# A three-mixer transformer block on one core: projections of the third stretch in program order, raw weights loaded a set ahead, and two sets of weights in memory that other data has left

## The chip, the cores and the metric

The kernel runs on one core of a Trainium2 chip. A time is the device time of one execution in microseconds. Of the kernel before, three executions were timed: 2087.23, 2089.68 and 2092.42 us, median 2089.68 us. One more execution was recorded by the profiler; all rows below come from it.

The engines are named as in the profile: PE multiplies matrices and transposes, DVE and ACT work on tiles element by element and empty PSUM, POOL works on tiles in SBUF, SP issues the DMAs.

## The reference, cut to what matters

The block takes 1024 tokens of width 1024. Its first part runs three mixers on the same normed input and merges them with gates; its second part is a gated MLP with a short convolution. Everything is float32.

```python
hn = rms_norm(x, norm_mix_g)
u = hn @ w_in                      # 1024 x 7864: MLA latents, forgetting attention, SSD, gates
y_a = mla_branch(u_mla, ...)       # latents -> q, k, v of 8 heads, rotary tail, chunk-causal softmax
y_b = fox_branch(u_fox, ...)       # q, k normed per head; scores plus differences of cumulated log-sigmoids
y_c = ssm_branch(u_ssm, ...)       # convolution, scan over chunks of 64, times silu(z)
merged = g0 * y_a + g1 * y_b + g2 * y_c
x = x + merged @ w_out
x = x + (silu(gate) * val) @ w_down          # gate, val = split(conv(rms_norm(x) @ w_up))
```

## The kernel before, in words

A float32 product is made of three products of halves: `split` (L142 and L143) writes the high half `h` with ACT and the rest `l` with DVE, and `mm3` (L167) sums high times high, high times low and low times high on PE. The stages follow each other on PE, and in most of them PE is the engine that never rests:

- norm and latents (to about 97 us), which leave the latents of the eight tiles of 128 tokens in `ch` and `cl`;
- MLA projections and forgetting-attention values (to about 226 us). For each token tile `t`: products `q` and `kv`, norms and rotary parts on DVE and POOL, then four groups of transposes (`tp`, L500), each emptied into `sh` by ACT (L503) and into `sl` by DVE (L504) and stored by SP (L507). `sh` and `sl` have two buffers each. Beside them run 16 value units `fxv` (8 token tiles, two sets of 256 columns), each emptied into the tile `fv` (one buffer) and stored (L519);
- what the change calls the third branch (226 to 424 us): four sets of 512 columns, in the order z (first half), forgetting-attention queries, keys, z (second half). `load512` loads a set as four raw pieces (tag `wr`, two buffers) and splits each into `w5h` and `w5l`; two sets fit. Then eight units per set, 24 matmuls of 512 columns each, into the PSUM tile `fx`. A z unit is emptied by a tanh and one DVE instruction (`zt`). A query or key unit takes a square on ACT, a reduction `fss`, thirteen small instructions for the reciprocal root and a product `fqn` on DVE, four transposes on PE, then `fsh` on ACT and `fsl` on DVE (one buffer each) and four stores. `gate_sums` (dt, decays, cumulated sums) and `down_sums` (sums of FFN down weights, on POOL, with loads and stores) lie in between;
- attention with fill-in gate projections, the scan, the merge and `w_out` (to about 1445 us);
- the FFN up projection (to about 1876 us): 22 pairs of column blocks, each as seven products of quarter blocks. `raws(i)` loads the two raw blocks of a pair into the tag `wr` (two buffers), POOL forms the sums S12 and S34 (L1417 to L1421), DVE and ACT split them, and PE runs the banks `ua`, `ub`, `uc`, `ud` (L1322). The right-hand sides need token sums T2, T3, T4, made one after the other in the tile `T3f`. The first four pairs are begun early;
- the down projection to the end.

The order of instructions on an engine is in most stages made by a scheduler in the compiler; a `manual_schedule` region keeps the named engines in the order in which the code is written. In the FFN, PE alone is kept so. In the third branch nothing was. SP issues its DMAs in one queue, and a DMA that waits holds up those behind it.

Of the kernel before, what the change touches and what calls it, by code (L numbers as in the profile page):

```python
# [11 lines left out]
F32 = mybir.dt.float32  # L12
# [30 lines left out]
def block_kernel(ctx: ExitStack, tc: tile.TileContext, x, positions, norm_mix_g, w_in, b_gate,  # L43
# [91 lines left out]
    def uid(s):  # L135
        cnt[0] += 1
        return f"{s}_{cnt[0]}"
# [188 lines left out]
    pmla = ExitStack()  # L326
# [5 lines left out]
    ch = [chp.tile([P, 5, P], F32R, name=f"ch{t}", tag=f"ch{t}") for t in range(NT)]  # L332
    cl = [chp.tile([P, 5, P], F32R, name=f"cl{t}", tag=f"cl{t}") for t in range(NT)]

    with ExitStack() as p0:
# [71 lines left out]
        upp = pmla.enter_context(TP("upp", 1, side="right"))  # L407
# [8 lines left out]
    def load_cols(pool, tag, c0, n, bufs):  # L416

        h = pool.tile([P, NK, n], F32R, name=uid(tag), tag=tag + "h", bufs=bufs)
        l = pool.tile([P, NK, n], F32R, name=uid(tag), tag=tag + "l", bufs=bufs)
        for k in range(0, NK, 2):  # L420
            raw = pool.tile([P, 2, n], F32, name=uid("raw"), tag=tag + "r", bufs=2)
            SY.dma_start(raw, w_inv[:, k:k + 2, c0:c0 + n])
            split(h[:, k:k + 2, :], l[:, k:k + 2, :], raw)
        return h, l

    with ExitStack() as pm:
        fvp = pm.enter_context(TP("fvp", 1))
# [6 lines left out]
        def rope(eng, dst, src, t, n):  # L434

            c = cos[:, t:t + 1, :].to_broadcast([P, n, 16])
            s = sin[:, t:t + 1, :].to_broadcast([P, n, 16])
            a, b = src[:, :, 0:16], src[:, :, 16:32]
            t1 = mp.tile([P, n, 16], F32, name=uid("rp1"), tag=f"rp1_{n}", bufs=1)
            t2 = mp.tile([P, n, 16], F32, name=uid("rp2"), tag=f"rp2_{n}", bufs=1)  # L440
            t3 = mp.tile([P, n, 16], F32, name=uid("rp3"), tag=f"rp3_{n}", bufs=1)
            t4 = mp.tile([P, n, 16], F32, name=uid("rp4"), tag=f"rp4_{n}", bufs=1)
            eng.tensor_mul(t1, a, c)
            eng.tensor_mul(t2, b, s)
            eng.tensor_mul(t3, a, s)
            eng.tensor_mul(t4, b, c)
            eng.tensor_sub(dst[:, :, 0:16], t1, t2)
            eng.tensor_add(dst[:, :, 16:32], t3, t4)

        vcols = [load_cols(fvp, "v", C_FQ + 1024, 256, 1)]  # L450
        for t in range(NT):

# [31 lines left out]
            kn = mp.tile([P, 8, 96], F32, name=uid("kn"), tag="kn")  # L484
# [11 lines left out]
            for src, col, dsts in ((qn, gq_col, (q_h, q_l)), (kn, gk_col, (k_h, k_l))):  # L496
                for g in range(2):
                    pt = tps()
                    for j in range(4):
                        T.transpose(pt[:96, j, :], src[:, 4 * g + j, :], ident)  # L500
                    sh = mp.tile([96, 4, P], F32R, name=uid("sh"), tag="sh")
                    sl = mp.tile([96, 4, P], F32R, name=uid("sl"), tag="sl")
                    A.activation(sh, pt[:96, :, :], AF.Copy, scale=col)  # L503
                    V.scalar_tensor_tensor(out=sl, in0=pt[:96, :, :], scalar=col, in1=f32(sh),  # L504
                                           op0=ALU.mult, op1=ALU.subtract)
                    for dst, st in zip(dsts, (sh, sl)):
                        SY.dma_start(dst[4 * g:4 * g + 4, :, t * P:(t + 1) * P].rearrange("h d s -> d h s"), f32(st))  # L507


        for c0 in (0, 256):  # L510
            if c0:
                vcols.append(load_cols(fvp, "v", C_FQ + 1024 + c0, 256, 1))
            vh, vl = vcols[-1]
            for t in range(NT):
                p = acc("fxv", "mv")[:, 0:256]
                mm3(p, tok(hnh, t), tok(hnl, t), lambda k: vh[:, k, :], lambda k: vl[:, k, :], NK)
                vt = fvp.tile([P, 4, P], F32R, name=uid("fv"), tag="fv", bufs=1)
                split(vt[:, :, 0:64], vt[:, :, 64:128], p.rearrange("p (h d) -> p h d", d=64))
                SY.dma_start(fv_d[t * P:(t + 1) * P, c0 // 64:c0 // 64 + 4, :], f32(vt))  # L519
    pmla.close()  # L520
# [18 lines left out]
    V.tensor_add(yv, small, b24.unsqueeze(1).to_broadcast([P, NT, 24]))  # L539
    V.scalar_tensor_tensor(out=yn, in0=yv, scalar=-1.0, in1=yv, op0=ALU.mult, op1=ALU.min)  # L540
    A.activation(e, yn, AF.Exp)
    V.tensor_scalar_add(rec, e, 2.0)
    V.reciprocal(rec, rec)
    V.tensor_mul(s_, e, rec)
    V.tensor_mul(s2, s_, s_)
    V.tensor_scalar_mul(q_, s2, 1.0 / 17)
    for c in (15, 13, 11, 9, 7, 5, 3):
        V.scalar_tensor_tensor(out=q_, in0=q_, scalar=1.0 / c, in1=s2, op0=ALU.add, op1=ALU.mult)
# [66 lines left out]
    with ExitStack() as px:  # L615
# [1090 lines left out]
```

## Time and profile before

| What | us |
|---|---|
| profiled execution, its time | 2090.6 |
| its span in the profile | 2088.9 |
| median of the three timed runs | 2089.68 |
| PE busy in the span | 2019.1 |
| DVE busy in the span | 1402.3 |
| ACT busy in the span | 952.7 |
| POOL busy in the span | 621.7 |

PE is busy for 97% of the span, so the idle time of PE, and the matmuls that run slowly after it, are all that a change of order can win. The table of windows gives, for a stretch of time, the busy time of each engine with its count of instructions, and the clock that PE was granted. The list of waits names what ended each idle stretch of an engine. A matmul of 512 columns is recorded as some 0.39 us long, but the next one starts before it ends; what counts is their pitch, the time from start to start.

### The profile page before, as it was taken

The numbers are of one execution on the slowest core, as the hardware profiler recorded it, in microseconds if no ns is written. First come the engines' busy times: TensorE is split into PE (matmuls) and PEld (weight loads), VectorE is DVE, ScalarE is ACT, GpSimd is POOL, SyncE is SP. The second block draws the span as 40 slices with busy tenths as digits, with TensorE's granted clock in tenths as the row PEclk, the third lists the DMA queues.
The fourth block names the chain that finished last, engine by engine and source line by source line (L and its number), as shares of the span: only waits on it lengthen the run. The fifth ranks groups of instructions, "written<-read, shape, count | busy, mean of one in ns | idle before, by whom it ended". The sixth has DMA issues, their size and how long they took to land.

```text
span 2088.9 us, 29138 instructions
## 1 busy us (share of the span) xinstructions
PE 2019.1 (97%) x10265; PEld 1684.8 (81%) x10265; DVE 1402.3 (67%) x2595; ACT 952.7 (46%) x1739; POOL 621.7 (30%) x606
## 2 busy tenths in 40 slices
PE   6999898999999999999999999999989999999999
PEld 6998687788888888788777888888768888878887
DVE  6687468456666777666987356557887766765665
ACT  5555222145565666554554223323444454444432
POOL 2454122322222222220000030002465455432765
PEclk9999999999999999999999999999999999999999
DMA  5067667754343554324442665431222222229675
GB/s 173 27 182 226 225 222 241 233 154 121 118 130 90 132 157 124 102 81 145 124 132 85 202 205 183 150 123 54 68 91 81 81 81 91 81 93 353 235 227 191
DMA packets 276650, 303.62 MB, mean 145 GB/s; under 512 B 19308, under 2 KB 209784, under 8 KB 276504
## 3 DMA queue, kind: packets, MB, share of 16 engines
q1 hardware_dynamic: 276504, 301.76, 46.7%
q8 instruction: 81, 1.33, 0.3%
q14 instruction: 65, 0.53, 0.1%
HBM read 209.03 MB, written 92.67 MB: 144 GB/s over the span
## 4 chain that ended last, share of the span: by engine, by line
PE 80%; DMA 8%; DVE 6%; ACT 2%; issue 2%; POOL 2%; SPq 0%; ACTq 0%; DVEq 0%; POOLq 0%
PE mm L796 17%; PE dn L1653 9%; PE ybr L167 8%; PE fx L167 5%; PE ua L1322 5%; PE uc L1322 4%; PE ud L1322 4%; PE wo L1368 4%; PE s L886 4%; PE tp L955 2%; PE ub L1322 2%; DMA att_d<-o 2%; PE cq L167 1%; PE q L167 1%; PE o L926 1%
## 5 line engine op out<-in xcount | busy, mean ns | idle before, releaser
L796 PE MATMUL mm<-hnh,wh 128*128 128x512 f32 x576 | 250.4, 435 | 0.0
L796 PE MATMUL mm<-hnh,wl 128*128 128x512 f32 x576 | 226.5, 393 | 0.0
L796 PE MATMUL mm<-hnl,wh 128*128 128x512 f32 x576 | 225.1, 391 | 0.0
L908 POOL TENSOR_SCALAR pm<-pm,rs 128x128 f32<-128x128 f32 (+7 forms) x128 | 107.7, 843 | 351.4 <-DVE rs L907 320.6
L1653 PE MATMUL dn<-dr,dr 128*128 128x512 f32 x592 | 182.3, 389 | 0.0
L961 DVE TENSOR_TENSOR ptl<-tp,pth 128x512 fp32r<-128x512 f32 (+1 forms) x160 | 101.4, 633 | 85.5 <-ACT pth L960 84.6
L891 DVE TENSOR_REDUCE nmx<-s 128x1 f32<-128x128 f32 (+2 forms) x192 | 105.7, 551 | 56.2 <-PE s L889 44.5
L901 ACT ACTIVATE pm<-s,nmx 128x128 f32<-128x128 f32 (+2 forms) x192 | 109.6, 575 | 55.5 <-DVE nmx L898 38.4
L1653 PEld LDWEIGHTS dn<-dr,dr 128*128 128x128 f32 x592 | 111.1, 188 | 22.9
L796 PEld LDWEIGHTS mm<-hnh,wl 128*128 128x128 f32 x576 | 108.1, 188 | 24.8
L796 PEld LDWEIGHTS mm<-hnl,wh 128*128 128x128 f32 x576 | 109.0, 189 | 18.4 <-issue 4.1
L796 PEld LDWEIGHTS mm<-hnh,wh 128*128 128x128 f32 x576 | 108.9, 189 | 17.8 <-issue 4.1
L960 ACT ACTIVATE pth<-tp 128x512 fp32r<-128x512 f32 (+1 forms) x160 | 88.1, 551 | 68.8 <-PE tp L955 68.0
L886 PE MATMUL s<-qk,qk 96*128 96x384 f32 (+5 forms) x480 | 117.6, 350 | 0.9 <-ACT pm L901 0.9
L1238 POOL TENSOR_TENSOR mg<-mg,gl 128x512 f32<-128x512 f32 x16 | 24.8, 1557 | 305.9 <-DVE gl L1235 305.8
L1653 PE MATMUL dn<-dr 128*128 128x512 f32 x296 | 115.3, 390 | 0.1
L142 ACT ACTIVATE wh<-wr 128x1024 fp32r<-128x1024 f32 (+1 forms) x47 | 43.0, 914 | 146.1 <-PE ybr L167 65.0
L167 PE MATMUL fx<-w5h,hnh 128*128 128x512 f32 x256 | 102.1, 403 | 7.6 <-ACT w5h L142 7.6
L143 DVE TENSOR_TENSOR dr<-dr,dr 128x1024 fp32r<-128x1024 f32 x52 | 76.0, 1465 | 49.2 <-ACT dr L142 47.1
L167 PE MATMUL fx<-w5h,hnl 128*128 128x512 f32 x256 | 101.6, 398 | 0.0
L167 PE MATMUL fx<-w5l,hnh 128*128 128x512 f32 x256 | 101.2, 397 | 0.0
L167 PE MATMUL ybr<-al,wh 128*128 128x512 f32 x256 | 99.2, 389 | 0.0
(469 smaller groups left out, 5822.5 us busy)
## 6 DMA issues: line engine op xcount, KB each, us to landing
dr<-act_d SPq DMA_DIRECT2D x99, 256.0 KB
wr<-in_ffn_w_up_dram SPq DMA_DIRECT2D x47, 512.0 KB
wr<-in_w_in_dram SPq DMA_DIRECT2D x36, 512.0 KB
g_d<-t SPq DMA_DIRECT2D x24, 512.0 KB
gl<-g_d SPq DMA_DIRECT2D x24, 512.0 KB
ws<-in_ffn_w_down_dram SPq DMA_DIRECT2D x22, 512.0 KB
wsum_d<-ws SPq DMA_DIRECT2D x22, 512.0 KB
act_d<-fa SPq DMA_DIRECT2D x22, 512.0 KB
```

The costliest lines, as they stand in the source:

```text
L143: return i, le.tensor_sub(l, src, f32(h))
L167: T.matmul(ps, a(k), b(k), start=(i == 0), stop=(i == n - 1))
L796: T.matmul(ps, a[:, k, :], b[half][:, k, :], start=(k == 0 and i == 0), stop=(k == NK - 1 and i == 2))
L886: T.matmul(ps[:, :w], q_[:, qs], k_[:, a:a + w], start=i_ == 0, stop=not last and i_ == len(o.passes) - 1)
L891: later(c + 0.1, lambda ps=ps, ci=ci, a=a, b=b: V.reduce_max(nmx[:, ci:ci + 1], ps[:, :b - a], axis=AX, negate=True))
L901: pss[ci][1][0] = later(c + 0.9 + 0.1 * ci, lambda ci=ci, a=a, b=b: A.activation(p_[:, a:b], pss[ci][0][:, :b - a], AF.Exp, bias=nb, accum ...
L908: G.tensor_scalar(p_[:, 0:n * P], p_[:, 0:n * P], rs[:, 3:4], 0.0, op0=ALU.mult, op1=ALU.add)
L960: later(c + 0.05, lambda th=th, pt=pt, off=off: A.activation(th[:, :off], pt[:, :off], AF.Copy))
L961: pl[0] = later(c + 0.6, lambda th=th, tl=tl, pt=pt, off=off: V.tensor_sub(tl[:, :off], pt[:, :off], f32(th[:, :off])))
L1322: T.matmul(ps, a, b, start=first and n == 0, stop=n == 11, skip_group_check=not first)
L1368: T.matmul(p, a, b, start=k == 0 and i == 0, stop=k == NK - 1 and i == 2)
L1653: T.matmul(ps[m], a[:, ts_], b[:, 512:], start=first_ and j == 0 and q == 0, stop=j == NFH - 1 and q == 2, skip_group_check=not first_)
```

## The change

Nothing that is computed changes. It has five parts.

1. Memory. The latents become four tiles of four token tiles each (`chA`, `chB`, `clA`, `clB`). From token tile 5 on, the split value weights of the second set are written into `chA` and `clA`, whose token tiles 0 to 3 have then been used. `fv` gets two buffers for the first eleven value units.
2. The first set of the third branch. Once the MLA up weights are free (`pup.close()`), a pool `zr` takes their place with four raw buffers for the first z set and four `fv` buffers for the last five value units. The raw pieces are loaded there before those units, and split into the first `w5` set, which lies where the value weights of the first set were, ahead of the branch.
3. The third branch runs in a region in which PE, DVE and ACT are kept in the written order. Its raw pieces now use the four buffers of the tags `wh` and `wl`; the raw pieces of set i+1 are issued at the start of set i, and one piece is split before every odd unit. The transposes of a query or key unit (`turned`) follow two units later; `fsh` and `fsl` have two buffers. `gate_sums` is a generator whose pieces are run one by one between units.
4. FFN: the raw blocks of odd pairs from pair 3 on are loaded into the memory of `T3f` (tag `T3f`), those of the others into `wr` as before.
5. FFN, pair 1: the product `ub` stands ahead of `ud`, not behind the second `uc`.

```diff
-    ch = [chp.tile([P, 5, P], F32R, name=f"ch{t}", tag=f"ch{t}") for t in range(NT)]
-    cl = [chp.tile([P, 5, P], F32R, name=f"cl{t}", tag=f"cl{t}") for t in range(NT)]
+    def four(n):
+        return chp.tile([P, 4, 5, P], F32R, name=uid(n), tag=n)
+    chs, cls = ([four(n + i) for i in "AB"] for n in ("ch", "cl"))
+    ch, cl = ([h[t // 4][:, t % 4] for t in range(NT)] for h in (chs, cls))
...
+    def load512(c0):
+        for k in range(0, NK, 2):
+            if c0 == C_Z:
+                raw = zrp.tile([P, 2, 512], F32, name=uid("raw"), tag="zr", bufs=4)
+            else:
+                raw = f32(fpl.tile([P, 2, 512], F32R, name=uid("raw"), tag=("wh", "wl")[k // 2 % 2]))
+            SY.dma_start(raw, w_inv[:, k:k + 2, c0:c0 + 512])
+            raws.append((k, raw))
...
         for t in range(NT):
+            if t == 5:
+                vcols.append(load_v(*(f32r_halves(four(n)) for n in ("chA", "clA")), 256))
...
+            heads_turn(t, qn, kn)
+        for i in range(NT + 3):
+            values(i % NT, i // NT * 256, fvp.tile([P, 4, P], F32R, name=uid("fv"), tag="fv", bufs=2))
+        pup.close()
+        zrp = pup.enter_context(TP("zr", 1, side="right"))
+        load512(C_Z)
+        for t in range(3, NT):
+            values(t, 256, zrp.tile([P, 4, P], F32R, name=uid("fv"), tag="fv", bufs=4))
     pmla.close()
...
+    for _ in range(NK // 2):
+        split512()
+    pup.close()
...
+        with tc.manual_schedule(engines={mybir.EngineType.PE, mybir.EngineType.DVE, mybir.EngineType.Activation}):
+            for i, which in enumerate((3, 0, 1, 4)):
+                wh, wl = w5[i]
+                for t in range(NT):
+                    if which != 4 and t == 0:
+                        load512({3: C_FQ, 0: C_FQ + 512, 1: C_Z + 512}[which])
+                    if which != 4 and t % 2:
+                        split512()
...
+                    mm3(p, tok(hnh, t), tok(hnl, t), lambda k: wh[:, k, :], lambda k: wl[:, k, :], NK)
+                    if which != 3 or t in (2, 3):
+                        next(gs, None)
+                    if waiting and waiting[0][0] <= units - 2:
+                        turned(*waiting.pop(0)[1:])
...
     def raws(i):
         out_ = []
-        for j in (i, i + NFF):
-            raw = fpl.tile([P, NK, P], F32, name=uid("wr"), tag="wr", bufs=2)
+        if i % 2 and i > 1:
+            two = t3p.tile([P, 2, NK, P], F32, name=uid("wr2"), tag="T3f")
+        for n, j in enumerate((i, i + NFF)):
+            if i % 2 and i > 1:
+                raw = two[:, n]
+            else:
+                raw = fpl.tile([P, NK, P], F32, name=uid("wr"), tag="wr", bufs=2)
...
         product(c0_, hS12, 0, *T1)
+        if n == 1:
+            b0 = bank("ub")
+            product(b0, hS12, 4, *T2)
         d0 = bank("ud")
         product(d0, hS34, 0, *T3)
...
         if n == 1:
             finish_pair(*plain)
-            b0 = bank("ub")
-            product(b0, hS12, 4, *T2)
```

Smaller edits: the rotary step uses two scratch tiles in place of four, and the squares of the key half are written into the tile `kn`, whose place they leave before `kn` is written.

What the compiler makes of it, at three places. The first is DVE at the end of the MLA stage. In the kernel before, the last token tile's four `sl` stand among the value units, then come pieces of `gate_sums` and three more `fv`, and the first split of the third branch follows 18 rows below this excerpt.

```order
L504 SCALAR_TENSOR_TENSOR sl_2701<-tp_2695,gq_col,sh_2700 96x512
L504 SCALAR_TENSOR_TENSOR sl_2712<-tp_2706,gq_col,sh_2711 96x512
L143 TENSOR_TENSOR fv_3101<-fxv_3076,fv_3101 128x4x64
L504 SCALAR_TENSOR_TENSOR sl_2723<-tp_2717,gk_col,sh_2722 96x512
L504 SCALAR_TENSOR_TENSOR sl_2734<-tp_2728,gk_col,sh_2733 96x512
L143 TENSOR_TENSOR fv_3130<-fxv_3105,fv_3130 128x4x64
L579 MEMSET neg 8x128
L603 COPY trim<-tri 128x128
L604 TENSOR_SCALAR trim<-trim 64x128
L143 TENSOR_TENSOR fv_3159<-fxv_3134,fv_3159 128x4x64
```

In the changed kernel, the same engine at the same place (L459 is the old L504):

```order
L143 TENSOR_TENSOR fv_3155<-fxv_3156,fv_3155 128x4x64
L459 SCALAR_TENSOR_TENSOR sl_2575<-tp_2569,gk_col,sh_2574 96x512
L459 SCALAR_TENSOR_TENSOR sl_2586<-tp_2580,gk_col,sh_2585 96x512
L143 TENSOR_TENSOR fv_3184<-fxv_3185,fv_3184 128x4x64
L459 SCALAR_TENSOR_TENSOR sl_2699<-tp_2693,gq_col,sh_2698 96x512
L459 SCALAR_TENSOR_TENSOR sl_2710<-tp_2704,gq_col,sh_2709 96x512
L459 SCALAR_TENSOR_TENSOR sl_2721<-tp_2715,gk_col,sh_2720 96x512
L459 SCALAR_TENSOR_TENSOR sl_2732<-tp_2726,gk_col,sh_2731 96x512
L143 TENSOR_TENSOR w5l_3222<-raw_3060,w5h_3221 128x1024
L143 TENSOR_TENSOR w5l_3222<-raw_3062,w5h_3221 128x1024
```

All value units are emptied first (`fv_3184` is the last), the last token tile's four `sl` come behind them, and the splits of the first z set behind those. On PE the four groups `tp` of that tile stand right in front of the first `fx`.

The second place is DVE in the query units of the third branch. Before, the pieces of two units and of two weight sets are mixed (`w5l_4196` is the set of the keys, `fss` belongs to a unit, `tot` and `F` to `gate_sums`):

```order
L569 TENSOR_TENSOR tot<-tot 128x8 x3
L571 TENSOR_TENSOR F<-pc_3564,tot 128x56
L663 TENSOR_REDUCE fss_3686<-fsq_3684 128x8
L607 COPY cum<-pd_3609 128x128
L665 TENSOR_SCALAR fv_740_3688<-fss_3686 128x8
L143 TENSOR_TENSOR w5l_4196<-raw_4205,w5h_4195 128x1024
L148 TENSOR_SCALAR rs_i_3691<-fv_740_3688 128x8
L151 TENSOR_SCALAR rs_v_3694<-fv_740_3688 128x8
L149 TENSOR_SCALAR fr_741_3690<-rs_i_3691 128x8
L143 TENSOR_TENSOR w5l_4196<-raw_4209,w5h_4195 128x1024
```

Now a unit is finished before the next begins, with one split between two units:

```order
L725 TENSOR_TENSOR fqn_3815<-fx_3718,fr_765_3797 128x512
L143 TENSOR_TENSOR w5l_3648<-raw_3573,w5h_3647 128x1024
L684 SCALAR_TENSOR_TENSOR fsl_3862<-tp_3856,fq_col,fsh_3861 128x512
L719 TENSOR_REDUCE fss_3871<-fsq_3869 128x8
L721 TENSOR_SCALAR fv_782_3873<-fss_3871 128x8
L148 TENSOR_SCALAR rs_i_3876<-fv_782_3873 128x8
```

`fsl_3862` belongs to the unit two before the one whose `fss` follows it.

The third place is PE in pair 1 of the FFN; each row is the first of twelve alike. `wh_15798` holds S12, `wh_15802` S34. Before:

```order
L1322 MATMUL uc_15826<-hnh_13478,wh_15798 128x512
...
L1322 MATMUL ud_15839<-cbh,wh_15802 128x512
...
L1322 MATMUL uc_15826<-hnh_13478,wh_15802 128x512
...
L1322 MATMUL ub_15879<-cbh,wh_15798 128x512
...
L1322 MATMUL ud_15839<-cbh,h_4699_15806 128x512
```

And now, where `wh_15785` is S12 and `wh_15789` is S34:

```order
L1371 MATMUL uc_15813<-hnh_13465,wh_15785 128x512
...
L1371 MATMUL ub_15826<-cbh,wh_15785 128x512
...
L1371 MATMUL ud_15839<-cbh,wh_15789 128x512
...
L1371 MATMUL uc_15813<-hnh_13465,wh_15789 128x512
...
L1371 MATMUL ud_15839<-cbh,h_4693_15793 128x512
```

The product that needs only S12 now stands ahead of the first that needs S34. From the end of the third branch to the FFN, the five engines' orders are the same in both kernels.

More of the change, by code (lines that the diff above doesn't have):

```diff
@@ new lines, in block_kernel, with heads_turn @@
+    raws = []
+    def load512(c0):
[6 more added lines that the diff above has]
+            raws.append((k, raw))
+    def heads_turn(t, qn, kn):
+        for src, col, dsts in ((qn, gq_col, (q_h, q_l)), (kn, gk_col, (k_h, k_l))):
+            for g in range(2):
+                pt = tps()
+                for j in range(4):
+                    T.transpose(pt[:96, j, :], src[:, 4 * g + j, :], ident)
+                sh = mp.tile([96, 4, P], F32R, name=uid("sh"), tag="sh")
+                sl = mp.tile([96, 4, P], F32R, name=uid("sl"), tag="sl")
+                A.activation(sh, pt[:96, :, :], AF.Copy, scale=col)
+                V.scalar_tensor_tensor(out=sl, in0=pt[:96, :, :], scalar=col, in1=f32(sh),
+                                       op0=ALU.mult, op1=ALU.subtract)
+                for dst, st in zip(dsts, (sh, sl)):
+                    SY.dma_start(dst[4 * g:4 * g + 4, :, t * P:(t + 1) * P].rearrange("h d s -> d h s"), f32(st))
@@ L495, in block_kernel @@
                          rq[:, 8:16].unsqueeze(2).to_broadcast([P, 8, 32]))
[L496 to L507, printed above, removed]
@@ L510, in block_kernel @@
[L510 to L519, printed above, removed]
@@ new lines, in block_kernel, with turned @@
+        gs = gate_sums()
+        waiting = []
+        def turned(which, t, qn):
+            pt = tps()
+            for j in range(4):
+                T.transpose(pt[:, j, :], qn[:, 2 * j:2 * j + 2, :].rearrange("p h d -> p (h d)"), ident)
+            col = (fq_col, fk_col)[which]
+            sh = xp.tile([P, 4, P], F32R, name=uid("fsh"), tag="fsh", bufs=2)
+            sl = xp.tile([P, 4, P], F32R, name=uid("fsl"), tag="fsl", bufs=2)
+            A.activation(sh, pt, AF.Copy, scale=col)
+            V.scalar_tensor_tensor(out=sl, in0=pt, scalar=col, in1=f32(sh),
+                                   op0=ALU.mult, op1=ALU.subtract)
+            for dst, st in zip(((fq_h, fq_l), (fk_h, fk_l))[which], (sh, sl)):
+                dv_ = dst.rearrange("(a b) d s -> b d a s", b=2)
+                for b in range(2):
+                    SY.dma_start(dv_[b, 0:64, :, t * P:(t + 1) * P], f32(st[64 * b:64 * b + 64, :, :]))
```

198 lines of the change are left out of this document (95 added, 103 removed).

## The prediction

> **What bounds the kernel now.** I read the page first, then a table of windows, then the waits of PE, and the timeline only where those pointed.
>
> ```profile
> span 2088.9 us, 29138 instructions
> PE 2019.1 (97%) x10265; PEld 1684.8 (81%) x10265; DVE 1402.3 (67%) x2595; ACT 952.7 (46%) x1739; POOL 621.7 (30%) x606
> ```
>
> PE rests for 70 us in all, so no reordering can win more than that and the slow matmuls that follow a rest. The change touches three stretches. In the windows the columns are the length, PE, PEld, DVE, ACT and POOL busy with their instructions, the granted clock, the DMA share and GB/s.
>
> ```profile
> 180.00:220.00 40.00, 32.76 (x256) 30.21 (x255) 23.29 (x53) 16.18 (x29) 10.54 (x18) 1.00 0.78 229
> 220.00:230.00 10.00, 4.28 (x10) 3.41 (x11) 7.70 (x19) 2.87 (x5) 0.00 (x0) 0.52 0.31 97
> 270.00:390.00 120.00, 111.48 (x519) 91.27 (x519) 94.61 (x281) 31.94 (x49) 35.65 (x28) 0.97 0.72 224
> 330.00:340.00 10.00, 8.71 (x41) 6.89 (x39) 5.72 (x18) 1.74 (x3) 3.18 (x3) 1.00 1.00 333
> 340.00:350.00 10.00, 5.42 (x15) 4.48 (x16) 9.72 (x28) 3.77 (x5) 2.73 (x3) 0.66 0.74 228
> 380.00:390.00 10.00, 7.35 (x36) 5.67 (x35) 9.59 (x19) 1.18 (x2) 5.11 (x4) 1.00 0.69 246
> 1475.00:1485.00 10.00, 5.80 (x19) 4.33 (x18) 9.96 (x10) 5.61 (x6) 5.24 (x3) 0.74 0.00 1
> 1485.00:1505.00 20.00, 20.00 (x86) 16.46 (x85) 15.83 (x13) 6.93 (x8) 7.35 (x6) 0.96 0.26 85
> 1505.00:1565.00 60.00, 54.05 (x230) 42.44 (x229) 46.82 (x37) 27.54 (x32) 38.21 (x22) 1.00 0.30 95
> 1565.00:1865.00 300.00, 300.00 (x1323) 247.94 (x1322) 210.35 (x191) 147.26 (x174) 145.25 (x91) 1.00 0.26 83
> ```
>
> PE is idle 7.2 and 5.7 us where the MLA stage ends, 8.5 us in the query and key units (270 to 390), and 4.2 and 6.0 us where the FFN begins. From 1565 on the FFN leaves PE no gap, so nothing is to be won there. The pitch of a warm matmul of 512 columns comes from the chain of waits, where 151 of them follow each other:
>
> ```profile
> 389.96 34.27 PE fx L167 x151
> ```
>
> That is 0.227 us each, 5.45 us for a unit's 24. With it the windows show what a rest costs afterwards. From 220 to 230, ten matmuls took 4.28 us where 2.27 would do: 2.0 us lost at a clock of 0.52. From 340 to 350, fifteen took 5.42 where 3.41 would do: 2.0 lost. From 1475 to 1505, 105 took 25.8 where 23.8 would do: 2.0 lost. After the 2.65 us rest from 380 to 390 the clock stood at 1.00, with nothing lost. So a long rest costs 2 us on top.
>
> The list of PE's waits, of 90 to 440 us and then of 1430 to 1620, says what ended the rests (total, times, longest):
>
> ```profile
> PE fx L167 <- ACT w5h L142: 7.6, 1, 7.6
> PE tp L673 <- DVE fv L665: 5.9, 1, 5.9
> PE fxv L167 <- DVE fv L143: 3.7, 4, 1.5
> PE tp L673 <- DVE fqn L669: 2.6, 1, 2.6
> ...
> PE ud L1322 <- DVE wl L143: 4.2, 1, 4.2
> PE ua L1322 <- ACT cg L1514: 2.6, 1, 2.6
> ```
>
> **Part 1: the end of the MLA stage.** 7.2 + 5.7 + 2.0 = 14.9 us stand there. The timeline shows the reason:
>
> ```profile
> 202.91 0.38 ACT L142 ACTIVATE fv<-fxv 128x256 fp32r<-128x256 f32 x1 [5.20 <-DMA fv_d<-fv]
> ...
> 224.34 0.38 ACT L142 ACTIVATE fv<-fxv 128x256 fp32r<-128x256 f32 x1 [2.77 <-DMA fv_d<-fv]
> 224.62 2.00 ACT L142 ACTIVATE w5h<-raw 128x1024 fp32r<-128x1024 f32 x2
> 226.02 2.35 DVE L143 TENSOR_TENSOR w5l<-raw,w5h 128x1024 fp32r<-128x1024 f32 x2
> ```
>
> A value unit has one `fv`, so each waits until the store of the last has landed, and the first split stands behind the last `fv` on ACT. With two and four buffers these waits go, and the raw z weights have arrived before. But the order of DVE shows what is late next: the last token tile's four `sl` and then the splits. This chain has lain under value units so far:
>
> ```profile
> 201.27 1.03 PE L500 MATMUL tp<-ident,qn 128*96 128x128 f32 x8
> ...
> 203.19 1.25 ACT L503 ACTIVATE sh<-tp,gq_col 96x512 fp32r<-96x512 f32 x2
> 205.25 1.16 SPq L507 DMA_DIRECT2D q_l<-sl  x2
> 208.41 1.52 DVE L504 SCALAR_TENSOR_TENSOR sl<-tp,gk_col,sh 96x512 fp32r<-96x512 f32 x2 [1.65 <-DMA q_l<-sl]
> ```
>
> The key half's `sl` has to wait for the store of the query half, since there are two buffers. From the first transpose to the last `sl` it takes 209.9 - 201.3 = 8.6 us, of which 1.3 were a wait of `sh` for the `fv` ahead of it on ACT, which goes: 7.3. The first split adds half of the 2.35: 1.2. PE itself works 2.1 us of these 8.5 (two rows of 1.03). So a rest of 6.4 us comes back, with 2.0 for the clock after it: 8.4. The part wins 14.9 - 8.4 = 6.5 us. The bounds: 2 us if the 2 MB of raw z weights, which now travel beside the stores (DMA share 0.78), delay them by 4.5 us; 12 us if the stores land so early that a rest of 3 us is left.
>
> [...]
>
> **Part 2: the third branch in written order.** 8.5 us of rests plus the 2.0 after the long one make 10.5. They come from DVE, on which two units and the next weights were mixed (second excerpt of the order): `tp` of L673 waits for `fv` of L665, the start of a chain of small instructions. Now `turned` leaves that chain two units of time, some 12 us: a unit takes PE 5.45 us and its transposes, which the next row prices.
>
> ```profile
> L673 PE MATMUL tp<-ident,fqn 128*128 128x128 f32 x64 | 10.1, 282 | 8.5 <-DVE fv L665 5.9 <-DVE fqn L669 2.6
> ...
> L143 DVE TENSOR_TENSOR w5l<-raw,w5h 128x1024 fp32r<-128x1024 f32 x16 | 20.2, 1265 | 18.9 <-ACT w5h L142 18.9
> L157 DVE TENSOR_TENSOR rs_t<-fr 128x8 f32<-128x8 f32 x48 | 16.5, 344 | 1.5
> L158 DVE TENSOR_TENSOR rs_t<-rs_t,rs_v 128x8 f32<-128x8 f32 x48 | 13.2, 274 | 1.3
> ...
> L159 DVE SCALAR_TENSOR_TENSOR fr<-rs_t,fr 128x8 f32<-128x8 f32 x48 | 8.0, 166 | 1.4
> ```
>
> 10.1 us over 16 units are 0.6, so PE needs 6.05 us a unit, 97 us for 16. DVE was busy 94.6 us between 270 and 390, where these units lay: 98% of that. It fits, barely, and the pieces of `gate_sums` come early in the stretch. I let 3 of the 10.5 us come back as rests and take 7.5, with bounds of 0 (all comes back) and 10.5. Written order also makes DVE wait at each split for a raw piece. That piece is issued a set, some 44 us, ahead, and four buffers hold a set, so these waits have cover; without it a piece would cost its transfer, 6.5 us by the row under the rivals, less the units that PSUM holds in store. The stores have two `fsh` and `fsl` now, which hides them as long as a round trip stays under two units.
>
> **Part 3: the start of the FFN.** 4.2 + 2.0 + 6.0 = 12.2 us. The first rest is that of `ud`, which waits for S34:
>
> ```profile
> 1480.04 2.35 DVE L143 TENSOR_TENSOR wl<-S,wh 128x1024 fp32r<-128x1024 f32 x2
> ...
> 1501.04 1.71 POOL L1417 TENSOR_TENSOR S<-wr 128x512 f32<-128x512 f32 x1 [7.09 <-DMA wr<-in_ffn_w_up_dram]
> ...
> 1537.56 1.62 POOL L1417 TENSOR_TENSOR S<-wr 128x512 f32<-128x512 f32 x1 [6.72 <-DMA wr<-in_ffn_w_up_dram]
> ```
>
> `ub`, 12 x 0.227 = 2.7 us, now runs in that rest, and 1.5 is left, short enough for the clock: 4.7 us won. The 6.0 us later come from raw blocks: POOL stands still until a pair's blocks arrive, as these wait in `wr` for the pair before. With the odd pairs in `T3f`, pair 3 can load once T4 is split, before `wr` is free, and each later pair has the other place. That stall goes; next is DVE, busy 46.8 of 60 us there and 9.96 of 10 ahead of it, so I let 1.2 of the 6.0 come back. The part wins 9.5, with bounds of 4.7 (the blocks help nothing, DVE was the limit) and 12.2.
>
> The smaller edits (two rotary scratch tiles, the squares in `kn`) order POOL, DVE and ACT instructions behind ones that stand before them on the same chain; I price them at nothing. The stages between have the same order as before and shift as a whole.
>
> **The sum.** 6.5 + 7.5 + 9.5 = 23.5 us. The profiled execution took 2090.6 us with a span of 2088.9, so it becomes 2067.1. It lies 0.9 above the median of the three runs, 2089.68, against which the result is measured: 2066. A measurement of this kernel can tell about 0.3%, 6.3 us, from no change.
>
> **The rivals.** First, all of it is won: stores land early and DVE keeps up. The upper bounds give 12 + 10.5 + 12.2 = 34.7 us: 2055. For it speaks that every rest named has its cause removed; against it, that the order puts a bare chain in front of the first `fx`. Chance 0.15.
>
> Second, the FFN blocks help nothing and DVE is the limit there: 6.5 + 7.5 + 4.7 = 18.7 us, 2071. For it speaks the 9.96 of 10 us of DVE ahead; against it the two POOL rows, which wait for a DMA and not for DVE. Chance 0.15.
>
> Third, DVE becomes the bound of the query and key units. L157 takes 344 ns and L159, of the same size, 166; L158 takes 274. Against 166 these excesses are 8.5 and 5.2 us over 48 each, 13.7 in all, and they come from DVE instructions held up while POOL runs `down_sums`. If the written order meets POOL as badly again, twice as much is lost: 13.7 us more on an engine that is 98% full, so the 7.5 of part 2 become -6 and the total 10: 2080. It decides when a unit's DVE work passes 6.05 us. Chance 0.12. [...]
>
> Fourth, slower: the stores of the query and key units become the bound through SP's one queue. ACT and DVE are now in written order, so a `fsl` whose buffer has not landed holds up the whole next unit.
>
> ```profile
> 329.87 6.52 DMA raw<-in_w_in_dram
> ...
> 371.76 4.34 DMA fk_l<-fsl
> ```
>
> A store takes 4.3 us; with two buffers it binds only if the round trip from `fsl` to landing passes 12.1 us. If it stood behind a raw piece and a down-weight load of the same size, 4.3 + 2 x 6.5 = 17.3 us, a unit would take 8.65 us, 2.6 more, 42 us over 16 units: 2066 + 42 = 2108. Below a round trip of 15 us the other gains still outweigh it. Against it: the same bytes go now at a share of 0.72. Chance 0.04.
>
> **Chances and range.** The forecast has 0.54. The first three rivals and the forecast are faster by over 6.3 us; of the third, a quarter (0.03) falls within 0.3%, and 0.03 of the forecast's tails too; slower is the fourth. That gives 0.90 faster, 0.06 same, 0.04 slower. The range from 2055 to 2081 takes in the first three rivals; the forecast's lower bounds together, 2 + 0 + 4.7 us, would be 2083 and are left out.
>
> **What would show it.** Part 1: no `fxv` waits for `fv`, the first `fx` starts near 219 us (225.7 now), waiting for `w5l` or `w5h`, and the waits of `sl` for the store `q_l` stand ahead of it. Part 2: from the first `fx` to the last some 190 us instead of 198.5, no `tp` wait of over 3 us, DVE near full. Part 3: `ud` waits about 1.5 us, the clock stays at 1.00, and POOL's L1417 no longer waits for `wr`. The forecast is wrong if the gap at the first `fx` is as long as before, if query and key units take over 6.3 us each, or if any stage between differs by more than 2 us.

## The result, and the profile after

The changed kernel takes 2073.23 us (median of 4 runs, 2070.47 to 2075.93) beside 2089.61 us before: a ratio of 0.9921, 95% interval 0.9900 to 0.9942. A second series gave 2071.27, 0.9907 (0.9886 to 0.9927); one of its 13 executions of the kernel before took 10963.94 us and is left out of the ratio, and the median of the other twelve is 2090.20 us. The gain is 16.4 and 18.9 us in the two; 23.5 had been forecast, and the range held the time. The profiled execution took 2071.0 us.

Of the page after, the line of busy times: PE does the same work, DVE is busy 23 us longer with as many instructions.

```profile
PE 2014.6 (97%) x10265; PEld 1684.3 (81%) x10265; DVE 1425.6 (69%) x2595; ACT 950.5 (46%) x1739; POOL 616.9 (30%) x606
```

The windows of the changed kernel, the FFN's shifted by the 15 us that it starts earlier (columns as before):

```profile
180.00:220.00 40.00, 33.89 (x266) 32.38 (x264) 27.80 (x64) 19.35 (x38) 16.62 (x35) 0.95 0.85 262
220.00:230.00 10.00, 9.26 (x29) 7.13 (x30) 5.07 (x6) 5.08 (x7) 0.00 (x0) 0.70 0.75 244
...
270.00:390.00 120.00, 117.36 (x557) 96.67 (x556) 98.37 (x286) 32.87 (x52) 38.53 (x28) 1.00 0.75 233
...
1460.00:1470.00 10.00, 8.51 (x37) 6.59 (x36) 9.96 (x10) 5.61 (x6) 5.24 (x3) 1.00 0.38 105
1470.00:1490.00 20.00, 15.50 (x67) 12.17 (x67) 19.96 (x14) 8.49 (x10) 16.84 (x9) 1.00 0.24 79
1490.00:1550.00 60.00, 57.87 (x255) 47.24 (x254) 52.31 (x42) 28.89 (x34) 37.46 (x22) 1.00 0.31 97
```

PE rests 6.9 us around the first `fx` (13.0 before) and 2.6 us in the query and key units (8.5 before). In the FFN the long rest of `ud` is gone, but a new one of 4.5 us stands in the 20 us behind it, where DVE is busy 19.96 of 20 and POOL 16.84. PE's waits name what is late now, from 90 to 440 us and then from 1410 to 1610:

```profile
PE tp L455 <- DVE sl L459: 4.5, 1, 4.5
...
PE fx L167 <- DVE w5l L143: 2.0, 2, 1.4
PE fx L167 <- ACT w5h L142: 1.7, 1, 1.7
...
PE uc L1371 <- ACT e L1585: 5.6, 2, 3.8
PE ud L1371 <- DVE wl L143: 1.5, 1, 1.5
PE ud L1371 <- ACT e L1587: 0.7, 1, 0.7
PE ua L1371 <- ACT cg L1563: 0.3, 1, 0.3
```

No `fxv` waits for `fv` any more, and `ud` waits the 1.5 us that were forecast. The wait of `uc` has grown from 1.7 to 5.6 us; its row in the kernel before (1430 to 1620):

```profile
PE uc L1322 <- ACT e L1533: 1.7, 2, 1.2
```

It waits for ACT's copy of the bank (L1585, the tile `e`), and this copy stands on ACT behind an `fa` of the pair before, which waits for POOL's `cv` (timeline of the changed kernel):

```profile
1483.58 1.24 ACT L1518 ACTIVATE fa<-cv,pc_f 128x1024 f32<-128x1024 f32 x1 [4.90 <-POOL cv L1599]
...
1486.63 0.58 ACT L1585 ACTIVATE e<-uc 128x512 f32<-128x512 f32 x1
```

The stages of every profiled execution, from starts of instructions in its trace: the first `fx`, from it to the last `fx`, when that last one starts, from there to the first `ybr` (attention, no order changed), from the first `ua` to the last `ud`, and from there to the end. Left out is the stretch from the first `ybr` to the first `ua`, 267.7 to 268.5 us in all of them. A row's name says where the kernel differs from the changed one; in its other stages it has the changed kernel's code.

| Kernel | us | first fx | fx | last fx | to ybr | FFN | rest |
|---|---|---|---|---|---|---|---|
| before | 2090.6 | 225.7 | 198.1 | 423.8 | 742.9 | 438.0 | 218.1 |
| changed | 2071.0 | 220.1 | 190.6 | 410.7 | 740.4 | 432.3 | 219.3 |
| changed, again | 2077.1 | 219.4 | 192.5 | 411.9 | 745.3 | 432.3 | 219.7 |
| no FFN part | 2076.9 | 217.5 | 192.6 | 410.1 | 743.1 | 437.3 | 218.0 |
| earlier ub alone | 2074.9 | 216.4 | 194.2 | 410.6 | 741.5 | 435.5 | 219.5 |
| blocks alone | 2073.0 | 217.4 | 192.2 | 409.6 | 742.0 | 434.8 | 218.1 |
| last tile's own memory | 2070.8 | 215.7 | 193.2 | 408.9 | 743.8 | 432.5 | 217.8 |
| no FFN sums | 2063.5 | 219.5 | 191.1 | 410.6 | 742.8 | 422.4 | 219.4 |
| scheduler's order | 2066.2 | 216.0 | 186.8 | 402.8 | 743.0 | 432.3 | 220.2 |
| same, one fsh, fsl | 2074.1 | 219.9 | 191.8 | 411.7 | 741.7 | 432.3 | 220.1 |
| same, late raws | 2071.6 | 215.9 | 191.9 | 407.8 | 744.0 | 432.3 | 219.0 |
| scheduler's order, own memory | 2063.9 | 214.9 | 187.8 | 402.7 | 740.3 | 432.7 | 220.3 |
| no down sums | 2064.2 | 216.6 | 187.9 | 404.5 | 740.9 | 432.3 | 218.5 |
| POOL in order | 2196.8 | 221.4 | 193.3 | 414.7 | 741.3 | 544.0 | 229.1 |

Two things are seen before any experiment is read. The attention, in which no instruction was moved, takes 740.3 to 745.3 us from one execution to the next: that scatter is larger than most differences asked for here, so the experiments are judged by their stage and not by one total. And parts 1 and 2 of the prediction, the end of the MLA stage and the third branch, belong together: of the kernels with the written order and all of POOL's work there, those that reach the first `fx` earlier tend to take longer to the last one (220.1 and 190.6 at one end, 216.4 and 194.2 at the other; POOL in order is the exception).

### The profile page after: what moved, and what is told of

Read it like the earlier page. It is cut to its first block, busy times and chain, and to the rows that moved or that the text cites. A ratio compares the mean times of both kernels' runs of the same rounds, so it can differ in the third digit from the quotient of the medians.

```text
span 2069.3 us, 29096 instructions
## 1 busy us (share of the span) xinstructions
PE 2014.6 (97%) x10265; PEld 1684.3 (81%) x10265; DVE 1425.6 (69%) x2595; ACT 950.5 (46%) x1739; POOL 616.9 (30%) x606
## 4 chain that ended last, share of the span: by engine, by line
PE 84%; DVE 7%; DMA 5%; ACT 2%; issue 2%; SPq 0%; POOL 0%; DVEq 0%; ACTq 0%; POOLq 0%
PE mm L840 17%; PE dn L1703 10%; PE ybr L167 8%; PE ua L1371 5%; PE fx L167 5%; PE ud L1371 5%; PE uc L1371 5%; PE wo L1417 4%; PE s L930 4%; PE tp L999 3%; PE ub L1371 2%; PE fxv L167 1%; PE cq L167 1%; PE o L970 1%; PE kv L167 1%
## 5 line engine op out<-in xcount | busy, mean ns | idle before, releaser
L167 PE MATMUL ybr<-ah,wl 128*128 128x512 f32 x256 | 98.3, 389 | 0.0
```

What stands on the lines that cost most here:

```text
L167: T.matmul(ps, a(k), b(k), start=(i == 0), stop=(i == n - 1))
```

## The experiments

**The changed kernel once more**, as the yardstick.

> The changed kernel itself, as the yardstick of this series. Theory and rival alike: 2073 us, a ratio to the kernel before of 0.992, with runs near 2070.5 or near 2075.5.

Measured: 2071.27 us (2067.35 to 2077.1), ratio 0.9907 (0.9886 to 0.9927). The six executions are spread over this range and do not fall into the two groups that were expected. The profiled one is the longest, and 4.9 of its 6.1 us over the first profile are the attention's scatter.

**Part 3 undone, and its halves apart.** The two edits of the FFN (raw blocks of odd pairs in `T3f`, and the earlier `ub`), undone together, or one at a time:

```
-        if i % 2 and i > 1:
-            two = t3p.tile([P, 2, NK, P], F32, name=uid("wr2"), tag="T3f")
...
+            raw = fpl.tile([P, NK, P], F32, name=uid("wr"), tag="wr", bufs=2)
...
-        if n == 1:
-            b0 = bank("ub")
-            product(b0, hS12, 4, *T2)
         d0 = bank("ud")
...
             finish_pair(*plain)
+            b0 = bank("ub")
+            product(b0, hS12, 4, *T2)
```

> The changed kernel with part 3 undone (raw blocks of all pairs in wr again, ub behind the first pair's end again); parts 1 and 2 stay. Theory (the parts add up, and part 3 is worth what the two traces show, 5.7 us up to the last ud, less 1.2 lost as the down projection begins): 4.5 us above the changed kernel, 2077.5. Rival (part 3 was worth its forecast of 9.5 and another stage lost the difference): 9.5 above, 2082.5.

> The changed kernel with the raw blocks of the odd pairs in wr again; the earlier ub stays. Theory (the blocks only turn POOL's wait for a transfer into a wait for DVE, POOL and ACT that slow each other): within 1.5 us of the changed kernel, PE waits about 6 us behind ua or uc between 55 and 130 us after the first ua, POOL's first sum of a pair waits for wr. Rival (the blocks win some 5 us, and the waits of uc came from the earlier ub): 5 us above the changed kernel, 2078.

> The changed kernel with ub behind the first pair's end again; the raw blocks of the odd pairs in T3f stay. Beside 437.3 us from the first ua to the last ud without both, 435.5 with the earlier ub alone and 432.3 with both. Theory (the chain over POOL, DVE and ACT of pairs 1 to 4 sets the last ud, and what the earlier ub wins comes back at uc): 432 to 433 us. Rival (each is worth its own): 434 us or more.

Measured: without both 2076.97 us, ratio 0.9944 (0.9925 to 0.9964), 5.7 above the yardstick; with the earlier `ub` alone 2074.43, 0.9927 (0.9909 to 0.9946), 3.2 above it; with the blocks alone 2073.0 in a single execution. The FFN takes 437.3 us without both, 435.5 with `ub`, 434.8 with the blocks, 432.3 with both, and 432.3 again in five other traces that have both (432.5 and 432.7 in two more). Undone together they cost about what the theory of parts that add up says (4.5 us in all were expected, 9.5 by the rival). The halves are read from one trace each; the stage without both took 437.3 us here and 438.0 in the kernel before, so a few tenths are open. The earlier `ub` is worth 1.8 us alone and 2.5 beside the blocks, the blocks 2.5 and 3.2. Both theories on the halves fell: the blocks are not worth nothing, and the earlier `ub` does not come back whole. Each is worth about half of what was forecast for it, 4.7 and 4.8. PE's waits in the kernel with the earlier `ub` alone show where that half went:

```profile
PE ub L1366 <- ACT wh L142: 2.9, 2, 1.6
PE ud L1366 <- DVE wl L143: 1.5, 1, 1.5
...
PE ub L1366 <- DVE wl L143: 1.1, 2, 0.6
PE uc L1366 <- ACT e L1580: 1.0, 1, 1.0
...
PE ud L1366 <- ACT e L1582: 0.7, 1, 0.7
```

The rest of `ud` is down to 1.5 us, but the later sums on POOL still come at the pace of the transfers into `wr` (the sum at 1484.31 us stands behind a wait of 6.94 us for one), and PE, which is earlier now, waits 4.0 us as `ub` for their splits (1.0 without both edits). Matmuls run slowly behind these waits (0.63 us each from 1492.67 us on, behind rests of 1.32 and 0.61; granted clock 0.94 from 1490 to 1550), so the 2.0 us that were forecast for the clock are not won either.

The 23 us by which DVE is busy longer come with the blocks: over the span DVE is busy 1404.5 us without both edits, 1403.7 with the earlier `ub` alone, 1426.2 with the blocks alone and 1425.6 with both, in 2595 instructions each. The next run shows with what DVE's instructions collide.

**The FFN without the sums on POOL.**

```
-        S12, S34 = sums(ri, rj)
-        hS12 = halves(S12)
-        hS34 = halves(S34)
+        hS12 = halves(rj)
+        hS34 = halves(ri)
```

> The changed kernel without the FFN's sums on POOL: a pair's two raw blocks are split as they are and used in place of S12 and S34, which leaves that part of the computation out. Theory (POOL's sums and DVE's instructions hold each other up once no sum waits for a block; the late sums and the late cv hold ACT's copy of uc): DVE's L1521 takes 1.2 to 1.3 us instead of 1.5 to 2.3 in the first pairs, no uc waits over 0.5 us, and from the first ua to the last ud 426 us instead of 432.3. Rival (DVE has too much of its own there): uc still waits 3 us or more, 430 us or more.

Measured in a single execution: 422.4 us for the FFN, and PE waits for nothing in it. The price of the sums on POOL is 9.9 us, more than the 6 of the expectation. It holds two things that this run does not separate: the sums' own place in the chain from the raw blocks to the splits, and what POOL and DVE do to each other. The second is seen in the groups of DVE in the same 80 us, first of the changed kernel, then without the sums (busy, mean ns of one):

```profile
L143 DVE TENSOR_TENSOR wl<-S,wh 128x1024 fp32r<-128x1024 f32 x9 | 15.7, 1743 | 1.2 <-ACT wh L142 1.2
L1521 DVE SCALAR_TENSOR_TENSOR fa<-cg,pc_f,fa 128x1023 f32<-128x1023 f32 x5 | 10.5, 2101 | 0.0
L1521 DVE SCALAR_TENSOR_TENSOR fa<-cg,pc_f,fa 128x1022 f32<-128x1022 f32 x4 | 9.2, 2309 | 0.0
```

```profile
L143 DVE TENSOR_TENSOR wl<-wr,wh 128x1024 fp32r<-128x1024 f32 x12 | 14.7, 1226 | 9.3 <-ACT wh L142 9.3
...
L1521 DVE SCALAR_TENSOR_TENSOR fa<-cg,pc_f,fa 128x1023 f32<-128x1023 f32 x5 | 6.4, 1284 | 0.0
L1521 DVE SCALAR_TENSOR_TENSOR fa<-cg,pc_f,fa 128x1022 f32<-128x1022 f32 x5 | 6.4, 1278 | 0.0
```

The same instruction takes 2.1 to 2.3 us beside POOL's sums and 1.28 without them, and POOL pays too (timeline of the changed kernel: two sums that are held up, and one that isn't):

```profile
1477.34 2.27 POOL L1469 TENSOR_TENSOR S<-wr 128x512 f32<-128x512 f32 x1
1479.58 2.27 POOL L1470 TENSOR_TENSOR S<-wr,S 128x512 f32<-128x512 f32 x1
...
1486.25 1.30 POOL L1466 TENSOR_TENSOR S<-wr 128x512 f32<-128x512 f32 x1 [2.70 <-DMA wr<-in_ffn_w_up_dram]
```

How much of the long wait for `cv` this makes can be estimated: POOL works without a pause from 1466.24 to 1483.55 us, eight instructions in 17.3 us; at 1.30 us each they would take 10.4, and the 6.9 us between are more than the 4.90 that `fa` waits.

Of what the two engines do to each other the trace shows these lengths and not how it comes about.

**POOL in program order in the FFN**, one word in the line that names the engines of the written order.

```
-    order2 = tc.manual_schedule(engines={mybir.EngineType.PE})
+    order2 = tc.manual_schedule(engines={mybir.EngineType.PE, mybir.EngineType.Pool})
```

> The changed kernel with POOL in program order in the FFN, so that a pair's Y and cv stand ahead of the next pair's sums. Theory (uc waits because cv stands behind the next pair's sums on POOL and ACT's queue stands behind cv): ACT's fa waits for cv no longer than 2 us, uc waits under 1 us, first ua to last ud 428 to 430 us, the time 3 us below the changed kernel. Rival (the sums then come too late for ub): ub waits for wh or wl, 432 us or more.

Measured: 2195.18 us, ratio 1.049 (1.047 to 1.0509). Theory and cure fell, and the rival holds. A pair's `cv` now stands ahead of the next pair's sums, the sums come after it, and `ub` waits for their splits in nearly every pair (PE's waits from 1410 to 1890 us, and a window in the middle):

```profile
PE ub L1371 <- DVE wl L143: 61.5, 17, 4.3
PE ub L1371 <- ACT wh L142: 4.2, 2, 2.5
```

```profile
1560.00:1860.00 300.00, 257.29 (x1023) 206.87 (x1022) 175.65 (x145) 115.90 (x134) 108.40 (x72) 0.91 0.21 65
```

Up to the end of the stage, at 1968 us, the first row grows to 72.2 us in 20 waits of 3.6; with the second row 76.4 us of rests stand where the changed kernel has 8.1. The FFN is 112 us longer, and the granted clock of 0.91 tells of the rest: matmuls run slowly behind the rests (1023 of them take 257.3 us in the window, 232 at the pitch of 0.227). So the scheduler's order, sums first, is the right side of a bad choice, and a `cv` for which `fa` waits 5 us is the cheaper harm.

**The last tile's halves in memory of their own.** The eight `sh` and `sl` of tile 7 go into latents, value halves and squares that are free by then; the order on PE, DVE and ACT stays.

```
+            if t == NT - 1:
+                c4 = four("chB").rearrange("p a b c -> p (a b) c")[0:96]
...
+                slots = [c4[:, 0:4], c4[:, 4:8], c4[:, 8:12], v2[:, 0:4], c4[:, 12:16], v2[:, 4:8],
+                         c4[:, 16:20], s1]
+            heads_turn(t, qn, kn, slots)
```

> The changed kernel with the last token tile's eight turned halves in memory that is free by then (latents of tiles 4 to 7, the value halves, the squares), so that none waits for a store; the order of every engine is the same. Theory (the rest ahead of the first fx is the chain of two-buffer rounds through the stores): the first fx starts 4 to 6 us earlier, at 214 to 216 us, sl and sh of tile 7 wait for no store, and the time is 5 us below the changed kernel, 2068. Rival (the raw z weights or the last transposes themselves set the start): the first fx at 219 or later, the time within 1 us of the changed kernel.

Measured: 2069.04 us, ratio 0.9898 (0.9879 to 0.9918), 2.2 us below the yardstick: between theory and rival, and with an interval that overlaps the yardstick's. The chain into the first `fx` of the changed kernel, from its chain of waits (start, length), is one of stores:

```profile
191.61 8.71 DMA q_h<-sh
...
201.11 3.34 DMA k_h<-sh
...
206.88 2.43 DMA q_l<-sl
...
210.26 5.31 DMA k_l<-sl
...
217.09 2.41 DMA q_l<-sl
...
220.35 1.14 DVE w5l L143
```

With own memory the wait of `tp` for `sl` is 1.1 us, here and in the last experiment below; in the eleven traces with the old chain it is 3.6 to 4.9. That rest is the stores'. The first `fx` starts at 215.7 (214.9 in the last experiment), and with the old chain at 215.9 to 221.4, so what the stores cost at the start is less clear than what they cost in rest. And the last `fx` starts at 408.9, only 0.7 to 3.0 us earlier than in six executions that have the written order and the old chain (409.6 to 411.9; a seventh has 414.7). PE's rests inside the third branch of this kernel say why:

```profile
283.67 0.66 PE L687 MATMUL tp<-ident,fqn 128*128 128x128 f32 x4 [2.03 <-DVE Fl L143]
...
368.77 0.50 PE L167 MATMUL fx<-w5l,hnh 128*128 128x512 f32 x1 [2.36 <-DVE w5l L143]
```

The same two rests are 0.52 and 1.42 us in the changed kernel, which comes 4.4 us later. PE waits for DVE at both places, and so an earlier start is paid back there.

**The third branch without the written order.**

```
-        with tc.manual_schedule(engines={mybir.EngineType.PE, mybir.EngineType.DVE, mybir.EngineType.Activation}):
+        with ExitStack():
```

> The changed kernel with the third branch's order left to the scheduler again (the early raw weights, the two fsh and fsl, the later transposes in the program stay). Theory (the written order carries part 2): the first fx to the last takes 197 us or more, tp waits again for fqn or fv, and the time is 5 us above the changed kernel. Rival (the early raws and the second buffers carry it): 191 to 194 us, the time within 2 us of the changed kernel.

Measured: 2066.81 us, ratio 0.9888 (0.9873 to 0.9903), and 186.8 us from the first to the last `fx`. The theory fell, and the rival was not bold enough: the written order carries none of part 2's gain, it costs 3.8 to 7.4 us of it (190.6 to 194.2 us in the eight traces with it and with all of POOL's work; without it 186.8 here and 187.8 in the last experiment). PE's only waits in this stretch are 1.7 us for `w5h` at its start and 0.7 later. What the scheduler did otherwise is seen in DVE's share of the query and key stretch, from 270 to 390:

```profile
270.00:390.00 120.00, 119.30 (x565) 98.31 (x565) 92.55 (x281) 29.30 (x48) 39.38 (x29) 1.00 0.74 231
```

DVE is busy 92.55 us there, 98.37 in the written order. The scheduler put four of the eight splits for the key and the last set ahead of DVE's work on the first query unit (at 263 to 270 us), where DVE has room (it is busy 18.8 of 35 us between 235 and 270 in the changed kernel); the written order puts all eight between the query and key units, at every odd one. That this is what makes the difference was not tested by itself.

**What then carries it: the second buffers or the early raw weights.** Both on the scheduler's order. In the first, `fsh` and `fsl` have one buffer; in the second, the raw weights of the last three sets go through the two `wr` buffers and are split at the set's start.

```
-            sh = xp.tile([P, 4, P], F32R, name=uid("fsh"), tag="fsh", bufs=2)
-            sl = xp.tile([P, 4, P], F32R, name=uid("fsl"), tag="fsl", bufs=2)
+            sh = xp.tile([P, 4, P], F32R, name=uid("fsh"), tag="fsh", bufs=1)
+            sl = xp.tile([P, 4, P], F32R, name=uid("fsl"), tag="fsl", bufs=1)
```

```
-                raw = f32(fpl.tile([P, 2, 512], F32R, name=uid("raw"), tag=("wh", "wl")[k // 2 % 2]))
+                raw = fpl.tile([P, 2, 512], F32, name=uid("raw"), tag="wr")
...
+                if which != 3:
+                    load512({0: C_FQ, 1: C_FQ + 512, 4: C_Z + 512}[which])
```

> The changed kernel with the third branch's order left to the scheduler, and one fsh and fsl again. Theory (the second buffers take the stores off DVE's path): fsl waits for its stores again, and the first fx to the last takes 3 us or more longer than the 186.8 us with two buffers. Rival (the raw weights a set ahead carry part 2): 186 to 188.5 us.

> The changed kernel with the third branch's order left to the scheduler, and the raw weights of its last three sets loaded through the two wr buffers and split at the set's start in the program, as in the kernel before; two fsh and fsl stay. Theory (the raw weights a set ahead carry part 2): fx waits again for w5h or w5l, the first fx to the last takes 190 us or more instead of 186.8. Rival (the second buffers and the later transposes carry it): 186 to 188.5 us.

Measured, a single execution each: 191.8 and 191.9 us instead of 186.8. In size both theories hold: each of the two is worth 5 us, in the scheduler's order and by one trace. The later `turned`, which both kernels keep, was not tested alone. (The kernel with one buffer even starts 3.9 us later and so has less to pay back.) DVE's groups, first with one buffer, then with late raws (idle before, by what):

```profile
L684 DVE SCALAR_TENSOR_TENSOR fsl<-tp,fk_col,fsh 128x512 fp32r<-128x512 f32 x8 | 6.0, 750 | 16.9 <-DMA fk_l<-fsl 11.3 <-ACT fsh L683 4.9 <-DMA fq_l<-fsl 0.7
```

```profile
L143 DVE TENSOR_TENSOR w5l<-raw,w5h 128x1024 fp32r<-128x1024 f32 x16 | 20.5, 1289 | 8.4 <-ACT w5h L142 8.4
```

In one detail the second expectation missed: no `fx` waits for the weights, PE waits 3.1 and 1.5 us as `tp` for DVE's small instructions, which stand behind those splits.

**The third branch without the down weights' sums on POOL.** The four subtractions are out, and the raw weights are stored in their place. A piece then takes two of the four `t4` buffers and not all of them, so this frees memory as well as POOL.

```
-            G.tensor_sub(s12[:, 0, :], w1[:, 1, :], w1[:, 0, :])
...
-            SY.dma_start(wsum_d[k, :, 0:2, :], s12)
+            SY.dma_start(wsum_d[k, :, 0:2, :], w1)
```

> The changed kernel without the four POOL sums of each piece of down weights that are made beside the third branch and the attention: the raw weights are stored in place of the sums (same loads and stores), which leaves that part of the computation out. Theory (DVE bounds the query and key units because POOL holds it up): L148, L151 and the instruction on fss take 170 to 230 ns instead of 370, DVE's share from 300 to 360 falls from 93% to about 80%, the late waits of fx for w5l and of tp for Fl go, and the first fx to the last takes 189 us instead of 191 to 194. Rival (DVE's own work bounds it): the durations or the waits stay, 191 us or more.

Measured in a single execution: 187.9 us from the first to the last `fx`, with the written order. The groups of the changed kernel, then without the sums:

```profile
L159 DVE SCALAR_TENSOR_TENSOR fr<-rs_t,fr 128x8 f32<-128x8 f32 x48 | 10.1, 210 | 1.6
...
L148 DVE TENSOR_SCALAR rs_i<-fv 128x8 int32<-128x8 int32 x16 | 5.9, 367 | 0.5
```

```profile
L159 DVE SCALAR_TENSOR_TENSOR fr<-rs_t,fr 128x8 f32<-128x8 f32 x48 | 8.0, 167 | 1.6
...
L148 DVE TENSOR_SCALAR rs_i<-fv 128x8 int32<-128x8 int32 x16 | 2.8, 172 | 0.5
```

The theory holds: DVE is busy 24.2 us of each 30 between 300 and 360 instead of 27.8 and 28.2, and of the late waits only 0.5 us for `w5l` is left. Against the 190.6 to 194.2 us of the written order, the sums on POOL cost 2.7 to 6.3 us here.

**Both gains together**, the scheduler's order and the last tile's own memory.

> The two gains together: the third branch's order left to the scheduler, and the last tile's turned halves in free memory. Theory (with DVE's order no longer fixed, the earlier start is kept): the first fx at 213 to 216 us, the last at 402 us or less, and the time is 7 us below the changed kernel, 2065, a ratio to the kernel before of 0.987. Rival (DVE gives the earlier start back here too): the last fx at 402.8 as with the scheduler's order alone, 2067.

Measured: 2066.57 us, ratio 0.9882 (0.9861 to 0.9902), the last `fx` at 402.7 where the scheduler's order alone has 402.8. The rival holds: the two do not add. These two kernels, at 0.9888 and 0.9882 with intervals that cover each other, are the best found, 4 to 5 us below the changed kernel's second series by the ratios; their intervals overlap with its own (0.9886 to 0.9927), and what is clear is the stage, 186.8 and 187.8 us against 190.6 to 194.2.

## Why the prediction was right, and where it was not

**Part 1**, forecast 6.5 us: right in cause and nearly in size. The first `fx` starts 5.6 us earlier in the profile, and 4.3 to 9.3 earlier in six more executions that have the parts 1 and 2, so the size is known to some 2.5 us only. The chain of `sl` and `q_l` stores took the place of `fv` as forecast, with a rest of 4.5 + 1.7 + 0.6 = 6.8 us (6.4 forecast) and slow matmuls behind it (clock 0.70). What the working missed is that the chain does not begin with the last tile: its stores wait for one another from tile 5 on, and the first of them takes 8.71 us behind the 2 MB of raw z weights, which left at 188.3 to 190.9 us: the delay that the prediction kept for its lower bound. Its upper bound sets nothing down for the clock behind a rest of 3 us, which no run shows: before, nothing was lost behind a rest of 2.65 us and 2.0 us behind one of 4.2, and in the changed kernel matmuls turned slow (0.63 us) behind one of 2.00.

**Part 2**, forecast 7.5 us: the size came out to the tenth, 198.1 - 190.6 (the 198.5 of the prediction runs to the end of the last `fx`), by luck and for a wrong reason. By luck, since six more executions of the same code give 3.9 to 7.0. The rests did come from DVE; the step that failed is the cure, that units kept apart by the written order take them away ("Now `turned` leaves that chain two units of time"). The scheduler, given the same buffers and loads, does better by 3.8 to 7.4 us. What carries most of the part is what the prediction named only as cover: the second `fsh` and `fsl` (5.0 us) and the raw weights a set ahead (5.1 us), beside 11.3 us that the stage gains in the scheduler's order. Whether the later `turned` has a share in the remaining 1.2, if the two add up, stays open. The 3 us set aside for DVE came back (2.6 of rest), and the third rival's mechanism, POOL holding DVE up, is seen in the durations (L148 takes 367 ns beside the sums on POOL, 172 without them); its price was 2.7 to 6.3 us of this stretch and not the 13.7 that it was given.

**Part 3**, forecast 9.5 us: 5.7, and this is the term that made the whole too large. Beside the 422.4 us without sums, where PE never waits, 15.6 us stood in this stage before and 9.9 are left. The first rest went as forecast (`ud` waits 1.5 us, the clock stays at 1.00 there), though its 4.7 us are only 1.8 to 2.5 by the end of the stage. The step that failed is "That stall goes; next is DVE ... so I let 1.2 of the 6.0 come back": 6.6 us of waits stand in their place. Once the blocks are early, POOL's sums run beside DVE's longest instructions, both slow down to some 2.3 us, DVE is busy 22 us longer for the same work, and ACT's copy of `uc` stands behind an `fa` that waits for POOL's `cv`. The second rival, with 4.7 us for this part, came nearer in size and half in reason: DVE is full, but because POOL works beside it, and the blocks do help, by 2.5 to 3.2 us.

**The sum.** Parts 1 and 2 end 13.1 us earlier in the profile, and 9.1 to 14.2 in six other executions with their code, beside 14.0 forecast. Part 3 gives 5.7 beside 9.5. What follows loses 1.2 us that the prediction did not have: the first steps of the down projection rest 2.0 us, now with a fall of the clock behind it. One execution cannot lay this to the change: the stage takes 217.8 to 220.3 us in the other executions that leave POOL's order alone, with such a fall in six of them and without it in five. The sum is 13.1 + 5.7 - 1.2 = 17.6; the profile's other 2 us lie in the attention, where no order changed and 5 us of scatter stand. The prediction's own sign of error, a stage between that differs by over 2 us, was met there by 2.5 us and was no sign: one execution before and one after cannot carry it.

## What to carry to other kernels

A rest that ends is worth its length less what the engine behind it can take: where DVE is nearly full (93% between 300 and 360 us here), ask first whether an earlier load or a second buffer relieves it, and write an order by hand only if the scheduler's own, with the same buffers, is slower. A stalled POOL was not idle room here, since its sums slowed DVE once both ran (an `fa` from 1.28 to 2.1 and 2.3 us). Before a stage's difference is believed, look at how far the stage scatters in executions of one kernel.

## What was not expected of the hardware

The clock's fall did not follow from the length of the rest. The same rest of `uc` stands in three executions of the same order; the rows are the first matmuls behind it, of the changed kernel, of its second series, and of the kernel with the last tile's own memory:

```profile
1487.26 0.50 PE L1371 MATMUL uc<-hnh,wh 128*128 128x512 f32 x1 [3.77 <-ACT e L1585]
1487.60 0.39 PE L1371 MATMUL uc<-hnl,wh 128*128 128x512 f32 x1
...
1488.53 0.39 PE L1371 MATMUL uc<-hnh,wl 128*128 128x512 f32 x1
```

```profile
1492.89 0.50 PE L1371 MATMUL uc<-hnh,wh 128*128 128x512 f32 x1 [3.71 <-ACT e L1585]
1493.23 0.39 PE L1371 MATMUL uc<-hnl,wh 128*128 128x512 f32 x1
...
1493.92 0.62 PE L1371 MATMUL uc<-hnl,wh 128*128 128x512 f32 x1
```

```profile
1488.35 0.79 PE L1379 MATMUL uc<-hnh,wh 128*128 128x512 f32 x1 [3.77 <-ACT e L1593]
1488.94 0.63 PE L1379 MATMUL uc<-hnl,wh 128*128 128x512 f32 x1
```

After 3.77 us the matmuls run on at 0.39 us, after 3.71 they turn slow 1 us later, after 3.77 again at once. And a rest of 2.00 us before the down projection was followed by a fall in the changed kernel, 1 us after its end:

```profile
1859.81 0.50 PE L1703 MATMUL dn<-wl,wh 128*128 128x512 f32 x1 [2.00 <-DVE wl L143]
...
1861.22 0.63 PE L1703 MATMUL dn<-wh 128*128 128x512 f32 x1
```

At the same place the kernel without the FFN's sums rests 1.01 and 0.80 us, one matmul apart, and its next matmuls are slow (0.63 us); the kernel without the down weights' sums rests 1.84 and 0.76 us, one matmul apart as well, and its next ones are not (0.40 us). So the 2.0 us set down for the clock behind a rest are an expectation over executions: in the FFN the three outcomes all end at 432.3 to 432.5 us, since PE, where it runs slower there, waits less behind it (its waits for ACT's copy as `uc` are 5.6 us in all in the first of the three, 4.1 in the second and 3.8 in the third).
